# Plain float32 projections, eight weight tiles in the ring, and the later conditioning on TensorE

## Chip, cores and metric

The kernel runs on one core of a Trainium2 chip. The metric is the device time of one execution in microseconds, as the median of several runs.

## What is computed

One layer of an encoder for 256 tokens of width 1024, in float32, with a conditioning vector c:

```python
h = rmsnorm(x) * (1 + scale1(c)) + shift1(c)
proj = h @ w_in                      # 1024 x 6688
x = x + gate1(c) * (concat(gdn_heads(proj), ssd_heads(proj)) @ w_out)   # 2048 x 1024
h = rmsnorm(x) * (1 + scale2(c)) + shift2(c)
x = x + gate2(c) * moe(h)            # 32 experts, top 4 of them for each token
out = rmsnorm(x)
```

The six conditioning vectors are c times a 1024 x 6144 matrix. The eight GDN heads (gated delta rule) and sixteen SSD heads work on chunks of the sequence, after a causal convolution over four tokens and a SiLU. Every expert has 12 MiB of weights, and all 32 are read.

## The kernel before

The front computes everything up to the router and the experts follow. Weights come in tiles of 1 MiB (128 partitions x 2048 columns). The names in `SLOTS` are 20 such places in SBUF; in the front five of them (`w0` to `w4`, `RING`) are a ring for weights, and the others hold working data. In the expert stage all twenty become one ring in the order of `SLOTS`: `fetch` loads expert weights into a place as soon as its last user is done. Two ring places that the front no longer needs are filled early (`Early`), six more after the GDN pairs, four after SSD, and the last eight when the front is over.

The front's weight work is a list of units, loaded in that order through SP's queue (`issue` loads the next one whose place is free). A unit `Ada` is 256 columns of the conditioning matrix, `Win` 256 columns of `w_in` with two jobs of 128 columns, `Wout` a part of `w_out` with two jobs. The first eight `Ada` units give shift1 and scale1, and two `Win` units go beside them. The other 16 `Ada` units (`pieces`) stand one after each of the next `Win` units.

The projections are in fp32r, with each operand split into a part that fp32r holds and the remainder, and three products for one: `Job.split` copies the weights (ScalarE, L323) and subtracts (GpSimd, L327, two instructions a job); h is split as `hs` (L675, L676) and y as `ys` (L1007, L1008, L1172, L1173). The multiplications of `Win` are on L363, those of `Wout` on L449. `Ada.run` has two ways: on TensorE (L386, the first eight) or on VectorE (L390, L392, the 16 pieces), eight operations of 128 x 256 each; `fill` puts them between the jobs, two at a time (`between`). `ada_cols` (L408) and `ada_rows` (L416) bring a piece's sums to columns or spread them over all partitions.

GDN (`gdn_pair`, four pairs of heads, 27 steps each) and SSD (`ssd`) are generators that yield after each step, and `run` calls the `filler` in between, so that half jobs of the projections stand between the steps (in the trace parts of a half job stand there too: the order on an engine is set when the program is built):

```python
for pr in range(4):
    run(gdn_pair(pr), (20, 32, 44, 52)[pr], 27)
...
run(ssd(), 62, 26)
```

After a job `post` does the convolution (`conv`: ScalarE L538 and L542, VectorE L540 three times and L545) or a gate (`gate2`), from one of two PSUM banks (`pmm`). `rsqrt` (L265 to L270) is a chain of eleven small VectorE operations; each pair has two of them, each SSD group one. `issue_after` queues instructions behind a given one on its engine. Ten small loads of biases and gates (`chores`) are issued from GpSimd's queue between the jobs.

Of the kernel before, what the change touches and what calls it, by code (L numbers as in the profile page):

```python
# [41 lines left out]
RING = 5  # L42

SLOTS = ("w0", "w1", "g", "odd", "c", "hh", "hl", "s2", "s1", "even", "xd", "s3", "w2", "w3", "w4", "wh", "wl", "yh",
# [4 lines left out]
def trunk_kernel(ctx: ExitStack, tc: tile.TileContext, x, c, ada_w, ada_b, norm1_g, norm2_g, w_in,  # L49
# [102 lines left out]
    whs, wls = slot("wh", "whs", FR), slot("wl", "wls", FR)  # L152
# [154 lines left out]
    def run_all(gen):  # L307
        for _ in gen:
            pass

    units, issued, done, oacc, free = [], [0], [0], [], set()
    class Job:
# [5 lines left out]
        def split(self, dst=None):  # L318
            u, i = self.unit, self.i
            w = u.half(i)  # L320
            h = turn("wh") * 1024
            self.wh, self.wl = (v[:, h:h + 1024] for v in dst or (whs, wls))
            self.first = S.activation(u.shaped(self.wh), w, AF.Copy)  # L323
            wh, wl = u.shaped(self.wh), u.shaped(self.wl)
            q = w.shape[1] // 2
            for r in (slice(0, q), slice(q, 2 * q)):
                self.last = (V if dst else G).tensor_tensor(wl[:, r], w[:, r], wh[:, r], op=OP.subtract)  # L327
            if i:
                u.w = None
                issue(u.tag)  # L330

        def mm(self, part):
            self.unit.mm(self, part)

# [3 lines left out]
    class Win:  # L338
# [9 lines left out]
        def half(self, i):  # L348
            return self.w[:, :, ts(i)]

        def shaped(self, v):
            return v.rearrange("p (k m) -> p k m", k=KT)
# [15 lines left out]
    class Ada:  # L368
# [9 lines left out]
        def run(self, tensor=True):  # L378

            a = self.a = part("c", (0, 256, 1536, 1792)[turn("adas", 4)], [256])  # L380
            if tensor:
                p = pg()
                for i in range(2):
                    for j in range(4):
                        k = 2 * j + i
                        self.last = T.matmul(p[32 * j:32 * j + 32, :256], cact[:, k:k + 1].to_broadcast([128, 32]), self.w[:, k],  # L386
                                 start=(i == 0), stop=(i == 1))
                S.activation(a, p[:, :256], AF.Copy)
            else:
                V.tensor_scalar(a, self.w[:, 0], cact[:, 0:1], None, op0=OP.mult)  # L390
                for k in range(1, KT):
                    V.scalar_tensor_tensor(a, self.w[:, k], cact[:, k:k + 1], a, op0=OP.mult, op1=OP.add)  # L392
                    if k % 2 and k < KT - 1:
                        yield
# [5 lines left out]
            self.over = quarter if tensor else ones  # L400
            self.w = None
            issue(self.tag)

    def ada_cols(u, dst):

        p = pg()
        for i in range(2):
            last = T.matmul(p[:, i:i + 1], u.a[:, ts(i)], u.over[:, 0:1], start=True, stop=True)  # L408
# [11 lines left out]
    class Wout:  # L420
# [9 lines left out]
        def half(self, i):  # L430
            return self.w[:, 2 * i:2 * i + 2]

        def shaped(self, v):
            return v.rearrange("p (k m) -> p k m", k=2)

        def mm(self, job, t):
            wh, wl = self.shaped(job.wh), self.shaped(job.wl)
# [36 lines left out]
    def fill():  # L474

        todo, sums, late = None, [], []
# [5 lines left out]
        def between():  # L482
            if sums:
                try:
                    next(sums[0][0])
                except StopIteration:
                    late.append([1, sums.pop(0)[1]])

        for j in jobs:
            if isinstance(j, Ada):  # L490
                sums.append((j.run(False), j))
# [3 lines left out]
            between()  # L495
# [7 lines left out]
            if n < len(real):  # L503
                real[n].split()
# [1084 lines left out]
```

## Time and profile before

| | us |
|---|---|
| median of 3 runs | 1420.82 (1420.29 to 1422.03) |
| the profiled execution | 1424.03 |
| its span, first to last instruction | 1422.2 |
| TensorE busy | 1272.2 |
| VectorE busy | 627.0 |
| ScalarE busy | 246.4 |
| GpSimd busy | 210.3 |

The profile is of one execution. PE is TensorE's multiplications, PEld its loads of the stationary operand, DVE VectorE, ACT ScalarE, POOL GpSimd, SP the engine whose queue issues most loads (SPq: an issue). Times stand in us from the start of the span, or ns where a row says so. A line such as L363 is a line of the kernel.

### The profile page before, as it was taken

The numbers are of one execution on the slowest core, as the hardware profiler recorded it, in microseconds if no ns is written. First come the engines' busy times: TensorE is split into PE (matmuls) and PEld (weight loads), VectorE is DVE, ScalarE is ACT, GpSimd is POOL, SyncE is SP. The second block draws the span as 40 slices with busy tenths as digits, with TensorE's granted clock in tenths as the row PEclk, the third lists the DMA queues.
The fourth block names the chain that finished last, engine by engine and source line by source line (L and its number), as shares of the span: only waits on it lengthen the run. The fifth ranks groups of instructions, "written<-read, shape, count | busy, mean of one in ns | idle before, by whom it ended". The sixth has DMA issues, their size and how long they took to land. (4 is left out here: it accounts for less than half of the span.)

```text
span 1422.2 us, 20287 instructions
## 1 busy us (share of the span) xinstructions
PE 1272.2 (89%) x8024; PEld 662.7 (47%) x8025; DVE 627.0 (44%) x1586; ACT 246.4 (17%) x464; POOL 210.3 (15%) x185
## 2 busy tenths in 40 slices
PE   5889698889888899999999999899998799999996
PEld 3777687788666333333333323233333333333332
DVE  6889998954686322323322322223222133222322
ACT  3343333342243000001000000001000010100001
POOL 3345443444464000000000000000000000000000
PEclk8989898999999999999999999999999899999997
DMA  9754455332628699999999999999999999999990
GB/s 340 240 168 162 155 159 177 110 129 86 240 90 319 276 424 423 422 424 424 424 423 422 424 424 423 423 423 424 424 424 424 424 424 424 381 423 424 422 409 33
DMA packets 130472, 469.78 MB, mean 330 GB/s; under 512 B 7900, under 2 KB 59216, under 8 KB 97568
## 3 DMA queue, kind: packets, MB, share of 16 engines
q1 hardware_dynamic: 128592, 464.58, 81.3%
q8 instruction: 95, 1.56, 0.4%
q0 software_dynamic: 1040, 1.67, 0.4%
q10 hardware_dynamic: 704, 1.64, 0.4%
q14 instruction: 41, 0.34, 0.1%
HBM read 466.22 MB, written 1.05 MB: 329 GB/s over the span
## 5 line engine op out<-in xcount | busy, mean ns | idle before, releaser
L1398 PE MATMUL pG<-w,xe 128*64 128x512 f32 (+1 forms) x1152 | 283.5, 579 | 21.3 <-DMA w<-in_moe_w_gu_dram 21.1
L1398 PE MATMUL pU<-w,xe 128*64 128x512 f32 (+1 forms) x1152 | 280.6, 574 | 0.0
L1426 PE MATMUL pY<-w,hTe 128*64 128x512 f32 x1024 | 225.2, 592 | 0.9 <-ACT hTe L1415 0.7
L1402 DVE TENSOR_SCALAR ga<-pG 128x512 f32<-128x512 f32 (+1 forms) x34 | 23.0, 676 | 411.8 <-PE pG L1398 411.8
L327 POOL TENSOR_TENSOR wls<-w,whs 128x512 fp32r<-128x512 f32 x128 | 170.0, 1350 | 216.5 <-ACT whs L323 205.8
L363 PE MATMUL mm<-hs,whs 128*128 128x256 f32 x800 | 174.1, 310 | 30.7 <-DVE t_c L540 13.1
L1398 PEld LDWEIGHTS pG<-w,xe 128*64 128x64 f32 (+1 forms) x1152 | 83.9, 135 | 163.1 <-issue 103.9
L1398 PEld LDWEIGHTS pU<-w,xe 128*64 128x64 f32 (+1 forms) x1152 | 87.9, 135 | 142.4 <-issue 139.9
L363 PEld LDWEIGHTS mm<-hs,whs 128*128 128x128 f32 x800 | 136.5, 207 | 37.7 <-issue 24.4
L1426 PEld LDWEIGHTS pY<-w,hTe 128*64 128x64 f32 x1024 | 71.8, 137 | 133.0 <-issue 127.9
L363 PE MATMUL mm<-hs,wls 128*128 128x256 f32 x400 | 121.8, 304 | 0.0
L1404 ACT ACTIVATE th<-ga 128x512 f32<-128x512 f32 (+1 forms) x34 | 21.1, 620 | 470.4 <-DVE ga L1402 470.4
L1437 DVE SCALAR_TENSOR_TENSOR ye<-pY,gs,g2p 128x512 f32<-128x512 f32 (+1 forms) x33 | 24.2, 734 | 172.7 <-PEq L1491 163.8
L323 ACT ACTIVATE whs<-w 128x1024 fp32r<-128x1024 f32 x66 | 69.8, 1058 | 84.6 <-PE mm L363 41.7
L363 PEld LDWEIGHTS mm<-hs,wls 128*128 128x128 f32 x400 | 82.8, 207 | 1.6 <-issue 0.7
L392 DVE SCALAR_TENSOR_TENSOR t_c<-w,cact,t_c 128x256 f32<-128x256 f32 x112 | 77.0, 697 | 0.2
L1370 DVE TENSOR_SCALAR xe<-pw,A,sh 128x64 f32<-128x64 f32 (+1 forms) x272 | 70.9, 337 | 0.5 <-PE pw L1366 0.5
L1438 ACT ACTIVATE yh<-ye 128x512 fp32r<-128x512 f32 (+1 forms) x35 | 21.2, 607 | 281.3 <-DVE ye L1437 277.3
L1357 PE MATMUL pw<-xt,P 128*64 128x512 f32 (+1 forms) x288 | 66.0, 592 | 0.0
L1395 PE MATMUL pG<-bias,id 96*64 96x512 bf16 (+1 forms) x72 | 14.6, 394 | 27.7 <-PEq L1491 27.7
L1360 ACT ACTIVATE xg<-pw 128x512 f32<-128x512 f32 (+1 forms) x34 | 19.9, 585 | 110.3 <-PE pw L1357 110.3
L1377 DVE TENSOR_SCALAR QT<-pU 128x256 fp32r<-128x256 f32 x32 | 13.6, 425 | 53.5 <-PE pU L1373 53.4
(444 smaller groups left out, 1345.9 us busy)
## 6 DMA issues: line engine op xcount, KB each, us to landing
w<-in_moe_w_gu_dram SPq DMA_DIRECT2D x256, 1024.0 KB, 19.4
w<-in_moe_w_down_dram SPq DMA_DIRECT2D x127, 1024.0 KB, 19.6
w<-in_w_in_dram SPq DMA_DIRECT2D x26, 1024.0 KB, 5.4
w<-in_ada_w_dram SPq DMA_DIRECT2D x24, 1024.0 KB, 5.3
w<-in_w_out_dram SPq DMA_DIRECT2D x8, 1024.0 KB, 4.8
xt<-in_x_dram ACTq DMA_DIRECT2D x1, 1024.0 KB, 5.3
w<-in_moe_w_down_dram SPq DMA_DIRECT2D x2, 512.0 KB, 17.8
out_dram<-o SPq DMA_DIRECT2D x4, 256.0 KB, 2.0
```

The source lines that it names most:

```text
L323: self.first = S.activation(u.shaped(self.wh), w, AF.Copy)
L327: self.last = (V if dst else G).tensor_tensor(wl[:, r], w[:, r], wh[:, r], op=OP.subtract)
L363: T.matmul(job.p, a[:, k], hs[b][:, k], start=(k == 0 and j == 0), stop=(k == KT - 1 and j == 2))
L392: V.scalar_tensor_tensor(a, self.w[:, k], cact[:, k:k + 1], a, op0=OP.mult, op1=OP.add)
L1357: T.matmul(p[self.rows(h), :self.wid], self.P[:, t], xt[:, t, self.cols(h)], start=(t == 0), stop=(t == 1))
L1370: V.tensor_scalar(xe[:, k], p[:, c0:c0 + cap], A2[:, k:k + 1], sh2[:, k:k + 1], op0=OP.mult, op1=OP.add)
L1398: self.last = T.matmul(dst, self.xe[:, k], self.w(k)[:, o:o + wid], start=False, stop=(k == KT - 1))
L1402: V.tensor_scalar(ga, self.pG, 7.0, None, op0=OP.min)
L1404: S.activation(th, ga, AF.Tanh, scale=0.851)
L1426: T.matmul(pY[self.rows(n)], self.hT[:, k % self.nt, self.rows(k // self.nt)], self.w(8 + k // 2)[:, k % 2, self.cols(n)], start=False, st ...
L1437: V.scalar_tensor_tensor(ye[:, c], self.pY[:, c], self.gs, g2p[self.cap][:, c], op0=OP.mult, op1=OP.mult)
L1438: S.activation(self.yh[:, c], ye[:, c], AF.Copy)
```

## The change

Both projections and the small one of L731 multiply float32 operands as they are: one multiplication where there were three, and no splits of weights, h or y. The weight tile of a unit is released after the last multiplication of its second job. The four places of splits (`hh`, `hl`, `wh`, `wl`) go; three become ring tiles (`RING` 8) and one holds h (`hT`). All 24 `Ada` units run on TensorE. Five ring places are filled early with expert weights, five more after the pairs. The ten small loads go through SP's queue.

```diff
-RING = 5
-
-SLOTS = ("w0", "w1", "g", "odd", "c", "hh", "hl", "s2", "s1", "even", "xd", "s3", "w2", "w3", "w4", "wh", "wl", "yh",
+RING = 8
+
+SLOTS = ("w5", "w6", "w7", "w0", "w1", "g", "odd", "c", "hT", "s2", "s1", "even", "xd", "s3", "w2", "w3", "w4", "yh",
          "yl", "xT")
...
-    whs, wls = slot("wh", "whs", FR), slot("wl", "wls", FR)
...
-        def split(self, dst=None):
-            u, i = self.unit, self.i
-            w = u.half(i)
-            h = turn("wh") * 1024
-            self.wh, self.wl = (v[:, h:h + 1024] for v in dst or (whs, wls))
-            self.first = S.activation(u.shaped(self.wh), w, AF.Copy)
-            wh, wl = u.shaped(self.wh), u.shaped(self.wl)
-            q = w.shape[1] // 2
-            for r in (slice(0, q), slice(q, 2 * q)):
-                self.last = (V if dst else G).tensor_tensor(wl[:, r], w[:, r], wh[:, r], op=OP.subtract)
-            if i:
-                u.w = None
-                issue(u.tag)
...
         def mm(self, part):
             self.unit.mm(self, part)
+            if part and self.i:
+                self.unit.release()
...
+        def release(self):
+            self.w = None
+            issue(self.tag)
...
         def mm_k(self, job, ks):
-            wh, wl = self.shaped(job.wh), self.shaped(job.wl)
             for k in ks:
-                for j, (a, b) in enumerate(((wh, 0), (wh, 1), (wl, 0))):
-                    T.matmul(job.p, a[:, k], hs[b][:, k], start=(k == 0 and j == 0), stop=(k == KT - 1 and j == 2))
+                T.matmul(job.p, self.w[:, k, ts(job.i)], hT[:, k], start=(k == 0), stop=(k == KT - 1))
...
-        def run(self, tensor=True):
...
-            if tensor:
-                p = pg()
-                for i in range(2):
-                    for j in range(4):
...
-                S.activation(a, p[:, :256], AF.Copy)
-            else:
-                V.tensor_scalar(a, self.w[:, 0], cact[:, 0:1], None, op0=OP.mult)
-                for k in range(1, KT):
-                    V.scalar_tensor_tensor(a, self.w[:, k], cact[:, k:k + 1], a, op0=OP.mult, op1=OP.add)
-                    if k % 2 and k < KT - 1:
...
-                if self.rows:
-                    o = 1024 + turn("rows") * 512
-                    self.parts = wbx[:, o:o + 512].rearrange("p (i n) -> p i n", i=2)
-                    S.activation(self.parts[:, 0], a, AF.Copy)
-                    V.tensor_tensor(self.parts[:, 1], a, self.parts[:, 0], op=OP.subtract)
...
+            p = pg()
+            for i in range(2):
+                for j in range(4):
+                    k = 2 * j + i
+                    self.last = T.matmul(p[32 * j:32 * j + 32, :256], cact[:, k:k + 1].to_broadcast([128, 32]),
+                                         self.w[:, k], start=(i == 0), stop=(i == 1))
+            S.activation(a, p[:, :256], AF.Copy)
             self.w = None
             issue(self.tag)
...
         p = pg()
-        for i in range(2):
-            T.matmul(p[:, :256], ones_r, u.parts[:, i], start=(i == 0), stop=(i == 1))
+        T.matmul(p[:, :256], quarter, u.a, start=True, stop=True)
...
             for i in range(2):
                 k = k0 + i
-                y = ys[self.kp][:, :, k % 4]
-                for j, (a, b) in enumerate(((0, wh), (0, wl), (1, wh))):
-                    T.matmul(oacc[self.nn][t], y[:, a, ts(t)], b[:, i], start=(k == 0 and j == 0),
-                             stop=(k == 15 and j == 2))
+                T.matmul(oacc[self.nn][t], ys[self.kp][:, k % 4, ts(t)], self.w[:, 2 * job.i + i], start=(k == 0),
+                         stop=(k == 15))
...
-        real = [None] * 4 + [j for j in jobs if isinstance(j, Job)]
-        real[4].split()
         n = 4
...
         for j in jobs:
             if isinstance(j, Ada):
-                sums.append((j.run(False), j))
+                j.run()
+                late.append([2, j])
                 continue
             if todo:
                 todo()
-            between()
...
-            if n < len(real):
-                real[n].split()
             if n >= 6 and n % 2 == 0 and chores:
-                with tc.issue_after(real[n].last.ins):
+                with tc.issue_after(last_load[0].ins):
                     chores.pop(0)()
-            between()
...
-    for u, i in zip(units, (4, 2, 1, 3, 4, 2, 3, 4)):
+    for u, i in zip(units, (2, 3, 4, 5, 6, 7, 2, 3)):
...
-    hT = slot("yl", "hT").rearrange("p (k m) -> p k m", k=KT)
+    hT = slot("hT", "hT").rearrange("p (k m) -> p k m", k=KT)
...
-        for j in pre[2 * i:2 * i + 2]:
-            if j.k == 0:
-                j.split(wx if i else (whs, wls))
         for j in pre[2 * i:2 * i + 2]:
             j.unit.mm_k(j, range(j.k, k))
             j.k = k
+        if k == KT:
+            j.unit.release()
...
-            last = (S.activation(hs[0][:, k], hT[:, k], AF.Copy),
-                    V.tensor_tensor(hs[1][:, k], hT[:, k], hs[0][:, k], op=OP.subtract))
...
-        for j, (a, b) in enumerate(((0, 0), (0, 1), (1, 0))):
-            T.matmul(p[0:32, :SEQ], wbh[:, a, k], hs[b][:, k], start=(k == 0 and j == 0), stop=(k == KT - 1 and j == 2))
+        T.matmul(p[0:32, :SEQ], wbd[:, k], hT[:, k], start=(k == 0), stop=(k == KT - 1))
...
-        yf = y.rearrange("p c h l -> p (c h l)")
-        V.tensor_tensor(yf, yf, p, op=OP.mult)
-        for hp in range(2):
-            yhl = ys[pr // 2][:, :, pr % 2 * 2 + hp]
-            S.activation(c4(yhl[:, 0]), y[:, :, hp], AF.Copy)
-            V.tensor_tensor(c4(yhl[:, 1]), y[:, :, hp], c4(yhl[:, 0]), op=OP.subtract)
+        V.tensor_tensor(ys[pr // 2][:, pr % 2 * 2:pr % 2 * 2 + 2].rearrange("p h (c l) -> p c h l", c=4), y,
+                        p.rearrange("p (c h l) -> p c h l", c=4, h=2), op=OP.mult)
...
-        chores.append(lambda: nc.gpsimd.dma_start(dst, ada_b[:, c0:c0 + dst.shape[1]].to_broadcast(list(dst.shape))))
+        chores.append(lambda: nc.sync.dma_start(dst, ada_b[:, c0:c0 + dst.shape[1]].to_broadcast(list(dst.shape))))
...
-        chores.append(lambda: nc.gpsimd.dma_start(bf[32 * i:32 * i + 32], src))
+        chores.append(lambda: nc.sync.dma_start(bf[32 * i:32 * i + 32], src))
...
-                    V.scalar_tensor_tensor(xT[:, ct], xT[:, ct], sng[:, ct:ct + 1], p[:, 0:256],
+                    V.scalar_tensor_tensor(ys[2 + g][:, ct % 4], xT[:, ct], sng[:, ct:ct + 1], p[:, 0:256],
                                            op0=OP.mult, op1=OP.mult)
-                    yhl = ys[2 + g][:, :, ct % 4]
-                    S.activation(yhl[:, 0], xT[:, ct], AF.Copy)
-                    V.tensor_tensor(yhl[:, 1], xT[:, ct], yhl[:, 0], op=OP.subtract)
...
+    for tag in ("yh", "yl"):
+        v = slot(tag, "ys").rearrange("p (q k m) -> p q k m", q=2, k=4)
+        ys += [v[:, 0], v[:, 1]]
...
-    fetch(len(W) + 6)
+    fetch(len(W) + 5)
```

## Rows read from the trace of the kernel before

**Rows 1.** The page: bandwidth in 40 equal slices of the span.
```profile
GB/s 340 240 168 162 155 159 177 110 129 86 240 90 319 276 424 423 422 424 424 424 423 422 424 424 423 423 423 424 424 424 424 424 424 424 381 423 424 422 409 33
```

**Rows 2.** Windows by stage: busy us and instructions of each engine.
```profile
core 0: us, PE busy (x) PEld busy (x) DVE busy (x) ACT busy (x) POOL busy (x), PEclk, DMA share, GB/s
...
49.20:72.00 22.80, 15.96 (x116) 15.04 (x116) 21.15 (x67) 7.06 (x17) 9.77 (x9) 0.85 0.59 189
72.00:166.00 94.00, 77.45 (x770) 70.78 (x769) 84.65 (x181) 33.67 (x68) 47.72 (x40) 0.91 0.50 164
166.00:244.00 78.00, 65.25 (x664) 58.90 (x664) 72.69 (x161) 29.79 (x58) 36.67 (x30) 0.91 0.51 163
244.00:317.00 73.00, 62.93 (x667) 56.80 (x666) 56.83 (x130) 27.94 (x55) 31.94 (x25) 0.96 0.36 120
317.00:369.00 52.00, 47.66 (x529) 41.22 (x527) 24.13 (x64) 15.87 (x32) 25.32 (x20) 0.97 0.33 112
369.00:437.00 68.00, 56.64 (x311) 42.31 (x309) 54.39 (x93) 24.77 (x40) 38.05 (x30) 0.95 0.48 178
437.00:452.00 15.00, 13.76 (x72) 10.21 (x70) 8.25 (x17) 6.95 (x19) 8.03 (x6) 1.00 0.76 293
452.00:476.00 24.00, 17.02 (x68) 8.29 (x70) 12.15 (x61) 2.25 (x7) 0.00 (x0) 0.79 0.57 233
476.00:496.00 20.00, 19.72 (x96) 7.01 (x94) 5.75 (x15) 1.83 (x3) 0.00 (x0) 1.00 0.96 386
```

**Rows 3.** TensorE's waits, 49.2 to 452 us: total, times, longest.
```profile
PE mm L363 <- DVE t_c L540: 13.1, 7, 4.0
PE mm L363 <- DVE pl L768: 6.8, 1, 6.8
PE mm L363 <- DVE rot L268: 5.9, 2, 4.5
PE g L1141 <- DVE t_s L1124: 5.4, 4, 2.2
PE iv L921 <- DVE t_s L936: 4.7, 6, 1.5
PE g L1002 <- DVE roy L270: 4.7, 3, 1.7
PE mm L363 <- DVE rkt L268: 4.4, 1, 4.4
```

**Rows 4.** The page: groups by line; busy us, mean ns, idle before.
```profile
L327 POOL TENSOR_TENSOR wls<-w,whs 128x512 fp32r<-128x512 f32 x128 | 170.0, 1350 | 216.5 <-ACT whs L323 205.8
...
L392 DVE SCALAR_TENSOR_TENSOR t_c<-w,cact,t_c 128x256 f32<-128x256 f32 x112 | 77.0, 697 | 0.2
```

**Rows 5.** Window of dense fp32r projections of 256 columns, L363 alone.
```profile
55.13:59.92 4.79, 4.59 (x39) 4.38 (x37) 1.00 1.00 329
```

**Rows 6.** Window of dense fp32r projections of 512 columns, L449 alone.
```profile
435.52:439.50 3.98, 3.82 (x17) 2.81 (x15) 1.00 1.01 415
```

**Rows 7.** Lines one by one: duration ns min/median/max, first and last start.
```profile
L1096 PE MATMUL g<-xe,t_s x4: 590/592/592, 376.9 to 378.2; 128*128 128x512 f32 x4
...
L540 DVE SCALAR_TENSOR_TENSOR t_c<-mm,cwg,t_c x72: 465/470/484, 61.3 to 282.6; 128x255 f32<-128x255 f32 x24, 128x254 f32<-128x254 f32 x24, 128x253 f32<-128x253 f32 x24
...
L270 DVE SCALAR_TENSOR_TENSOR roy<-rot,roy x12: 147/160/1214, 155.1 to 366.7; 128x4 f32<-128x4 f32 x12
```

**Rows 8.** Timeline of SP's queue around the start of the experts.
```profile
439.69 15.96 SPq L87 DMA_DIRECT2D w<-in_moe_w_gu_dram  x8
475.97 0.39 SPq L87 DMA_DIRECT2D w<-in_moe_w_down_dram  x1
```

**Rows 9.** Timeline: a conditioning piece on TensorE, and a pair's end.
```profile
36.95 1.07 PE L386 MATMUL g<-w,cact 128*32 128x256 f32 x16
...
306.36 1.29 POOL L327 TENSOR_TENSOR wls<-w,whs 128x512 fp32r<-128x512 f32 x1 [3.00 <-ACT whs L323]
...
306.51 1.17 DVE L265 TENSOR_SCALAR roy<-vv 128x4 int32<-128x4 int32 x1
```

More of the change, by code (lines that the diff above doesn't have):

```diff
@@ L304, in trunk_kernel @@
     sh2 = const.tile([128, KT], FT)
-    def run_all(gen):
-        for _ in gen:
-            pass
     units, issued, done, oacc, free = [], [0], [0], [], set()
@@ L346, in load @@
             self.w = load(win_src[:, :, self.c0:self.c0 + 256], [KT, 256], self.tag, self in loads[:10])
[L348 to L352, printed above, removed]
+        def release(self):
+            self.w = None
+            issue(self.tag)
         def mm(self, job, part):
@@ L376, in load, with run @@
             self.w = load(ada_src[:, :, self.c0:self.c0 + 256], [KT, 256], self.tag, self in loads[:10])
-        def run(self, tensor=True):
+        def run(self):
             a = self.a = part("c", (0, 256, 1536, 1792)[turn("adas", 4)], [256])
-            if tensor:
-                p = pg()
-                for i in range(2):
-                    for j in range(4):
-                        k = 2 * j + i
-                        self.last = T.matmul(p[32 * j:32 * j + 32, :256], cact[:, k:k + 1].to_broadcast([128, 32]), self.w[:, k],
-                                 start=(i == 0), stop=(i == 1))
-                S.activation(a, p[:, :256], AF.Copy)
-            else:
-                V.tensor_scalar(a, self.w[:, 0], cact[:, 0:1], None, op0=OP.mult)
-                for k in range(1, KT):
-                    V.scalar_tensor_tensor(a, self.w[:, k], cact[:, k:k + 1], a, op0=OP.mult, op1=OP.add)
-                    if k % 2 and k < KT - 1:
-                        yield
-                if self.rows:
-                    o = 1024 + turn("rows") * 512
-                    self.parts = wbx[:, o:o + 512].rearrange("p (i n) -> p i n", i=2)
-                    S.activation(self.parts[:, 0], a, AF.Copy)
-                    V.tensor_tensor(self.parts[:, 1], a, self.parts[:, 0], op=OP.subtract)
-            self.over = quarter if tensor else ones
+            p = pg()
[5 more added lines that the diff above has]
+            S.activation(a, p[:, :256], AF.Copy)
             self.w = None
@@ L407, in ada_cols @@
         for i in range(2):
-            last = T.matmul(p[:, i:i + 1], u.a[:, ts(i)], u.over[:, 0:1], start=True, stop=True)
+            last = T.matmul(p[:, i:i + 1], u.a[:, ts(i)], quarter[:, 0:1], start=True, stop=True)
         V.tensor_tensor(dst, p[:, 0:2], col("ab", 48)[:, u.c0 // 128:u.c0 // 128 + 2], op=OP.add)
@@ L428, in load, with release @@
             self.w = load(wout_src[:, 4 * self.kp:4 * self.kp + 4, self.nn * 512:self.nn * 512 + 512], [4, 512], self.tag, True)
[L430 to L434, printed above, removed]
+        def release(self):
+            self.w = None
+            issue(self.tag)
         def mm(self, job, t):
-            wh, wl = self.shaped(job.wh), self.shaped(job.wl)
             k0 = 4 * self.kp + 2 * job.i
@@ L474, in fill @@
     def fill():
-        todo, sums, late = None, [], []
+        todo, late = None, []
         jobs = [j for u in units[KT + 2:] if not isinstance(u, Early) for j in (u.jobs or [u])]
-        real = [None] * 4 + [j for j in jobs if isinstance(j, Job)]
-        real[4].split()
         n = 4
[L482 to L487, printed above, removed]
         for j in jobs:
             if isinstance(j, Ada):
-                sums.append((j.run(False), j))
+                j.run()
+                late.append([2, j])
                 continue
@@ L516, in finish_ada @@
         u = Ada(c0, None)
-        u.rows = kind is ada_rows
         u.finish = lambda: kind(u, dst)
@@ L631, in trunk_kernel @@
         issue(f"w{i}")
-    hs = [slot(tag, "hs", FR).rearrange("p (k m) -> p k m", k=KT) for tag in ("hh", "hl")]
     pre = [j for u in units[KT:KT + 2] for j in u.jobs]
@@ L639, in trunk_kernel @@
         j.p, j.k = p[:, :SEQ], 0
-    wx = [slot(tag, "wx", FR) for tag in ("s2", "g")]
     def pre_run(i, k):
-        for j in pre[2 * i:2 * i + 2]:
-            if j.k == 0:
-                j.split(wx if i else (whs, wls))
         for j in pre[2 * i:2 * i + 2]:
@@ L654, in trunk_kernel @@
         for i, u in enumerate(ua):
-            run_all(u.run())
+            u.run()
             if 2 * k2 + i == 6:
@@ L722, in trunk_kernel @@
     wbx = slot("xd", "wbh", FR)
-    wbh = wbx[:, 0:512].rearrange("p (a k m) -> p a k m", a=2, k=KT)
-    with tc.issue_after(last[0].ins):
-        S.activation(wbh[:, 0], wbd, AF.Copy)
-    with tc.issue_after(last[1].ins):
-        V.tensor_tensor(wbh[:, 1], wbd, wbh[:, 0], op=OP.subtract)
     p = pg()
     for k in range(KT):
-        for j, (a, b) in enumerate(((0, 0), (0, 1), (1, 0))):
-            T.matmul(p[0:32, :SEQ], wbh[:, a, k], hs[b][:, k], start=(k == 0 and j == 0), stop=(k == KT - 1 and j == 2))
+        T.matmul(p[0:32, :SEQ], wbd[:, k], hT[:, k], start=(k == 0), stop=(k == KT - 1))
     bd = fr.tile([32, 4, 2, 64], FT, name="bd", tag="rot", bufs=3)
@@ L819, in gdn_pair @@
         kT, qT, vT = (pair_tile(pr, n) for n in ("kT", "qT", "vT"))
-        rg = wbx[:, 512:1024].rearrange("p (i n) -> p i n", i=2)
+        rg = wbx[:, 0:512].rearrange("p (i n) -> p i n", i=2)
         for i, E in enumerate((V, G)):
```

5 lines of the change are left out of this document (removed).

## The prediction

> **What bounds the kernel now.** I read the bandwidth line of the page first: from about 480 us on the transfers run at 422 to 424 GB/s to the end [rows 1]. The expert stage is a stream of weights and the edit doesn't touch it, so it can only start earlier or later. The load queue shows which: its eight first-round loads of expert weights are issued by 455.65 us, and the next is issued at 475.97 us, when expert 0 has used up its first tile [rows 8]; the DMA share in between is 0.57 and then 0.96 [rows 2]. All 20 tiles are full before the experts start. So the end moves one for one with the end of the front, and loading 14 tiles early in place of 12 buys nothing.
>
> Next the windows of the front, 49.2 to 452 us (402.8 us) [rows 2]. TensorE is busy 339.7 us of it and idle 63.1. In the three stages from 72 to 317 VectorE is busy 214 of 245 us; from 317 to 369, where no conditioning piece is left, 24 of 52, and TensorE's idle share falls from 16% to 8%. The waits say who holds it: the seven shown, 45.0 us, all end with VectorE, most of them in front of a projection whose PSUM bank waits for a convolution or for the small operations queued ahead of it [rows 3]. The front is therefore a TensorE program held up by a full VectorE queue, in which GpSimd also has 170 us of weight splits [rows 4].
>
> **TensorE's added work.** The price of the two forms comes from dense stretches at the full clock. 39 fp32r multiplications of 256 columns start in 4.79 us, 0.12 us each [rows 5]; 17 of 512 columns in 3.98 us, 0.234 each [rows 6]. A float32 multiplication stands as two instructions: the four of L1096 (two multiplications, 512 columns) start from 376.9 to 378.2 us, three steps of 0.43 us [rows 7]. No row shows 256 columns on a full stationary tile. In proportion it is 0.214 us an instruction; an upper bound is 0.24, twice the fp32r step. I take 0.214, since the 512-column row leaves nearly nothing fixed per instruction.
>
> - Input projections: 52 jobs of eight k steps. 24 x 0.12 = 2.88 us becomes 16 x 0.214 = 3.42: +0.54, in all +28.
> - Output projection: 16 jobs. 12 x 0.234 = 2.81 becomes 8 x 0.428 = 3.42: +0.61, in all +10.
> - The 32-column projection of L731: 24 x 0.12 to 16 x 0.214, +0.5.
> - Sixteen pieces of conditioning on TensorE: 16 instructions took 1.07 us in the first eight pieces at full clock [rows 9], so 16 x 1.0 = +16. Four 32-column strips run side by side there, hence so little.
> - The eight row pieces spread with float32 in place of two fp32r: +0.2 each, +1.5.
>
> Sum: +56 us of TensorE time. Nothing of TensorE's own work goes away.
>
> **What is taken from the others.** VectorE loses the 112 multiply-adds of L392, 77 us [rows 4], the sixteen L390 that open the pieces, and the remainder subtractions of h, y and the row pieces: at least 77 of the 322 us that it is busy from 49.2 to 452 [rows 2]. GpSimd loses the whole of L327, 170 us. ScalarE loses the 66 copies of L323 and gains 16 short ones; it is never busy for half of a stage [rows 2], so neither counts.
>
> The splits cost more than their own time. VectorE's 4-element L270 takes 0.16 us at the median and 1.21 at worst, but L540, which reads PSUM, only 0.465 to 0.484 [rows 7]; at 306.4 us an L265 that works on 4 elements took 1.17 us just as L327 was running on GpSimd [rows 9]. Eleven such operations in a row stand at each end of a pair, and TensorE waits 4.7 us in front of L1002 and 5.9 and 4.4 in front of projections behind them [rows 3], 15 us in all. With no L327 they should be near their medians; what GpSimd keeps (its shares of rg, eg and ra) is a few microseconds a pair.
>
> The Trainium skill (SBUF — State Buffer, the part on the two sides and the shared port pair) says that VectorE and GpSimd have one port pair in common, that whoever starts first holds it for a whole instruction, and that the other is blocked fully; the rows on L270 and L540 agree. By that rule the 15 us of waits at the pair ends go; were the stretch something else, they would stay, and the sum would be +7 and not -8.
>
> **What TensorE can get back.** First the idle 63 us. Then the clock: its mean in the six stages before 437 us is 0.85, 0.91, 0.91, 0.96, 0.97 and 0.95 [rows 2], which makes 54 us at 1.2 GHz. Much of that is the idle time itself; taking half of it as work, which then took twice as long as it would, 13 us are lost. Together 76 us.
>
> How much returns decides the sign. With VectorE at 24 of 52 us but GpSimd still splitting, the stage from 317 to 369 us kept 8% idle [rows 2]. That is the bound from above: 33 us of idle in some 400, and 5 of clock. The bound from below is nothing left. After the edit the convolutions are still there, some 55% of VectorE in the pairs, but the pair ends lose their stretched operations and each half job in between covers 1.7 us in place of 1.4. I take 10 us of idle and 2 of clock left: 64 come back. 56 - 64 = -8.
>
> **What costs nothing, and under what cover.** Eight ring tiles: in the first slice the loads already run at 340 GB/s [rows 1] and their order stays, and after 49.2 us no wait for a load is among the seven [rows 3]. Were a load late, TensorE would stand for its 5 us. A tile is now released by its last multiplication, not by its split, so it is held about a job (3.4 us) longer; three more tiles cover that. The ten small loads move from GpSimd's queue to SP's. There each stands behind loads that wait for a tile; who needs them (bias parts, row pieces) comes jobs later. If one were late, it would hold a VectorE addition, and all convolutions behind it. The wait of a piece for two jobs, not one, before its columns are used delays nothing that is read before the front's end. Dropping the split of h takes a ScalarE and a VectorE step out of the first stage, but the four early jobs are longer by 0.54 each, which the +28 holds.
>
> **Sum.** The profiled execution took 1424.0 us (span 1422.2), 3.2 over the median 1420.8. 1424 - 8 = 1416, so 1413 as a median. A change within 0.2% (2.8 us) can't be told from none.
>
> **Rivals.**
>
> 1. TensorE becomes the bound and its idle time stays (slower). If pairs keep the 8% of the stage from 317 to 369, 38 of 76 us come back: 56 - 38 = +18, 1439. It decides from 56 us on, that is when more than 20 of the 76 are left. For it: that stage had little VectorE work and was still not full. Against: it had GpSimd's splits. Chance 0.25 for anything that ends slower this way, most of it near +8 to +12.
> 2. Everything comes back, and gaps too short to show as idle (a projection starts some 0.1 us late after a small multiplication) are hidden under the longer instructions: -20 to -25, 1396 to 1401. Chance 0.13.
> 3. The gain is eaten: no change, 1418 to 1424. The pair ends keep half of their 15 us (4.7, 5.9 and 4.4 [rows 3]), because L270 and its like stay stretched beside GpSimd's other work or queue behind convolutions: -8 + 7.5. Chance 0.12.
> 4. The price of 256 columns is the upper bound: 0.026 x 16 x 52 = +21 on the forecast, 1434. The rows for 512 columns speak against it. Chance 0.08. The Trainium skill (FP8 and Floating Point Precision, on true FP32) counts four passes through the array; by four fp32r steps of 0.12 that is 0.48 us for 256 columns, this rival's price, while L1096's 0.856 us for 512 is less than four times 0.234.
>
> **How the numbers follow.** The forecast holds 0.42, with a range of its own from 1405 to 1419 (0.40 of it faster, 0.02 same). Rival 1 is 0.22 slower and 0.03 same, rival 3 is 0.09 same, 0.02 faster and 0.01 slower, rival 2 all faster, rival 4 all slower. Faster 0.40 + 0.13 + 0.02 = 0.55, same 0.14, slower 0.31. The range of eight in ten reaches from the second rival to the middle of the first: 1397 to 1432.
>
> **What would show it.** Right: projections at 0.21 us an instruction with 832 of them in the input projections; no L327; L270 near 0.16 us at its mean; TensorE idle 10 to 20 us between 50 and 450, clock 0.97 or more; SP's first load of the second round near 468 us in place of 475.97. Wrong: instructions of 0.24 us, or idle over 20 us behind convolutions; then that load comes after 476. If the experts start earlier and the total doesn't follow, the step from the front to the end was wrong.

## The result and the profile after

The changed kernel takes 1396.06 us at the median of four runs (1392.94 to 1398.35), the kernel before 1420.74 (1420.29 to 1422.03): a ratio of 0.9817, with a 95% interval of 0.98 to 0.9834. The forecast was 1413, its own range 1405 to 1419. By its number what came is the second rival, "everything comes back", at 1396 to 1401, and it lies 1 us under the low end of the whole range. The profiled execution took 1398.35 us, its span 1396.5.

First the bandwidth line of the changed kernel's page, in slices of 34.9 us (35.6 before). It answers to [rows 1]:

```profile
GB/s 340 277 237 139 180 190 182 122 91 116 216 211 197 422 425 424 424 423 422 424 424 424 424 424 423 425 424 424 422 424 424 417 423 424 372 423 423 422 394 31
```

The full stream of about 424 GB/s starts one slice earlier and is as fast as before. So the gain lies ahead of it. The windows of the changed kernel by stage, with the columns of [rows 2]:

```profile
core 0: us, PE busy (x) PEld busy (x) DVE busy (x) ACT busy (x) POOL busy (x), PEclk, DMA share, GB/s
...
49.20:72.00 22.80, 22.80 (x121) 17.11 (x120) 12.55 (x58) 6.45 (x20) 0.62 (x1) 1.00 0.95 331
72.00:166.00 94.00, 93.79 (x864) 72.27 (x864) 56.02 (x160) 25.76 (x65) 4.50 (x3) 1.00 0.58 193
166.00:244.00 78.00, 77.96 (x719) 59.67 (x717) 40.94 (x112) 18.32 (x45) 3.58 (x3) 1.00 0.53 173
244.00:317.00 73.00, 72.93 (x676) 58.39 (x675) 36.70 (x102) 16.35 (x41) 5.66 (x5) 1.00 0.30 102
317.00:345.00 28.00, 27.84 (x214) 20.81 (x213) 10.29 (x33) 3.78 (x10) 0.00 (x0) 1.00 0.25 83
```

The second number of a row is its length, the next TensorE's busy time: 0.5 us of 295.8 are left idle, at the full clock (2.4 GHz) throughout. Before, TensorE had 0.85 to 0.97 of the clock here and idle time in every stage [rows 2]. GpSimd, busy for 126 us of the four stages from 49.2 to 317 us before, is busy for 14. What is left of TensorE's waits, from 49.2 to 425 us:

```profile
PE g L1167 <- ACT x1T L1165: 0.7, 1, 0.7
PE g L937 <- DVE roy L269: 0.4, 2, 0.2
PE g L1072 <- DVE t_s L1055: 0.3, 1, 0.3
```

Of the seven waits of [rows 3], 45.0 us, one is left, at a tenth: L937 is the old L1002, which waited 4.7 us and now waits 0.4. From 49.2 to 345 us TensorE's own work sets the front's length.

To compare kernels whose stages have moved, one window is taken in all that follows: from 49.2 us to the first instruction of the routing tables (the first L1349 of the kernel before, 462.36 us; in each other kernel up to 0.4 us before the same instruction). The row of the kernel before, then of the changed kernel:

```profile
49.20:462.36 413.16, 348.87 (x3149) 300.31 (x3148) 328.48 (x748) 147.70 (x290) 197.49 (x158) 0.93 0.48 164
```

```profile
49.20:434.62 385.42, 383.06 (x2966) 275.81 (x2964) 206.78 (x600) 86.95 (x221) 22.85 (x20) 1.00 0.52 181
```

The front is 27.7 us shorter with 34.2 us more of busy TensorE in it. The load queue's first load of the second round is at 448.35 us in place of 475.97 [rows 8]:

```profile
448.35 0.39 SPq L87 DMA_DIRECT2D w<-in_moe_w_down_dram  x1
```

### The profile page after: what moved, and what is told of

Its sections match the earlier page's. It is cut to its first block, busy times and chain, and to the rows that moved or that the text cites. A ratio compares the mean times of both kernels' runs of the same rounds, so it can differ in the third digit from the quotient of the medians.

```text
span 1396.5 us, 19286 instructions
## 1 busy us (share of the span) xinstructions
PE 1306.4 (94%) x7792; PEld 634.9 (45%) x7793; DVE 494.2 (35%) x1417; ACT 176.4 (13%) x379; POOL 34.7 (2%) x47
## 5 line engine op out<-in xcount | busy, mean ns | idle before, releaser
L342 PE MATMUL mm<-hT,w 128*128 128x256 f32 x800 | 202.6, 394 | 0.0
L1323 PEld LDWEIGHTS pG<-w,xe 128*64 128x64 f32 (+1 forms) x1152 | 83.3, 135 | 164.4 <-issue 101.0
L342 PEld LDWEIGHTS mm<-hT,w 128*128 128x128 f32 x800 | 145.6, 193 | 27.3 <-issue 7.2
L487 DVE SCALAR_TENSOR_TENSOR t_c<-mm,cwg,t_c 128x255 f32<-128x255 f32 (+2 forms) x72 | 34.5, 479 | 21.6 <-ACT t_c L485 20.6
L364 PE MATMUL g<-w,cact 128*32 128x256 f32 x384 | 33.5, 443 | 7.2 <-DMA w<-in_ada_w_dram 4.9
L1375 PE MATMUL acc<-yh,QT 64*128 64x512 f32 (+1 forms) x148 | 33.5, 430 | 3.2 <-ACT yh L1363 3.2
L1285 ACT ACTIVATE xg<-pw 128x512 f32<-128x512 f32 (+1 forms) x34 | 19.9, 585 | 109.6 <-PE pw L1282 109.6
L1320 PEld LDWEIGHTS <-id 96*64 96x64 bf16 (+1 forms) x144 | 5.9, 106 | 56.5 <-PEq L1416 52.5
L1282 PEld LDWEIGHTS pw<-xt,P 128*64 128x64 f32 (+1 forms) x288 | 17.1, 135 | 30.8 <-issue 30.1
```

The costliest lines, as they stand in the source:

```text
L342: T.matmul(job.p, self.w[:, k, ts(job.i)], hT[:, k], start=(k == 0), stop=(k == KT - 1))
L487: V.scalar_tensor_tensor(acc[:, s:], p[:, :SEQ - s], wc(3 - s), acc[:, s:], op0=OP.mult, op1=OP.add)
L1282: T.matmul(p[self.rows(h), :self.wid], self.P[:, t], xt[:, t, self.cols(h)], start=(t == 0), stop=(t == 1))
L1323: self.last = T.matmul(dst, self.xe[:, k], self.w(k)[:, o:o + wid], start=False, stop=(k == KT - 1))
L1375: T.matmul(dst, self.QT[n % 2][half_, t], part[half_, i * w:(i + 1) * w], start=False, stop=part is self.yl, skip_group_check=True)
```

## The experiments

Three theories of why so much came back. (A) VectorE lost the multiply-adds of the conditioning pieces. (B) GpSimd lost the subtractions of the split, which had stretched VectorE's work. (C) The longer float32 projections cover the gaps. Times are medians; ratios are to the kernel before, measured side by side (its medians there: 1420.3 to 1421.4).

**The pieces alone.** The kernel before, its 16 later pieces on TensorE, splits kept:

```
...
             if isinstance(j, Ada):
-                sums.append((j.run(False), j))
+                run_all(j.run())
+                late.append([2, j])
                 continue
```

> The kernel before with one part of the change alone: the 16 later pieces of the conditioning on TensorE; splits and the ring of five stay. Three theories of why 83 us of TensorE's time came back. (A) VectorE: with the multiply-adds of the pieces gone, its queue no longer holds TensorE. Then idle time of 49 to 450 us falls from 63 to under 20 us, TensorE has 16 us more to do, and the time falls by 25 to 35 us, to 1386 to 1396. (B) GpSimd: the subtractions of the split stretch VectorE's operations through a shared resource. They are still there, so over 40 us of idle time stay and the time is 1415 to 1435. (C) Cover: the longer float32 projections hide the gaps. They are not there either: 1420 to 1437.

Measured: 1413.96 us, 0.9942 (0.9924 to 0.9961). The front's row:

```profile
49.20:457.04 407.84, 364.09 (x3391) 302.43 (x3388) 261.73 (x609) 148.71 (x296) 190.01 (x156) 0.94 0.48 167
```

VectorE is 67 us less busy, and TensorE still has 44 us of idle time, where (A) wanted under 20 and (B) over 40. The time is 1 us under (B)'s range. A queue that is a fifth emptier does not end the waits.

**The pieces back.** The changed kernel with the pieces on VectorE in their old places (the old branch of `run`, its steps put between the half jobs):

```
             if isinstance(j, Ada):
-                j.run()
-                late.append([2, j])
+                if True:
+                    sums.append((j.run_v(), j))
...
                 continue
```

> The changed kernel with the 16 later pieces back on VectorE, in the places they had before; projections in plain float32, eight ring tiles. TensorE has 16 us less to do than in the changed kernel, VectorE about 90 us more (some 290 of 376). (A) VectorE's load made the idle time: 35 us or more of it return, 1412 to 1430. (B) and (C): with no subtraction on GpSimd, or with the longer projections as cover, idle time stays under 8 us and the time falls by 10 to 16 us, to 1380 to 1388.

Measured: 1376.26 us, 0.9677 (0.964 to 0.9714), 20 us faster than the changed kernel (4 us more than (B) and (C) allowed), and the fastest version here that leaves nothing of the computation out. Its front, and the multiply-adds in its lines of VectorE from 49 to 470 us (busy us, mean ns, idle before):

```profile
49.20:413.97 364.77, 360.42 (x2706) 266.65 (x2704) 248.81 (x725) 80.47 (x205) 21.92 (x20) 1.00 0.55 189
```

```profile
L362 DVE SCALAR_TENSOR_TENSOR t_c<-w,cact,t_c 128x256 f32<-128x256 f32 x111 | 53.1, 479 | 1.1
```

(A) falls: with the pieces on VectorE TensorE is idle for 4.3 us only. The same instruction took 697 ns on average before [rows 4]; here it takes 479. The pieces were never a load of 77 us; 24 of that was waiting inside the instruction.

**No subtractions.** The kernel before, all multiplications kept, the remainders of the later weights zero:

```
...
-            for r in (slice(0, q), slice(q, 2 * q)):
-                self.last = (V if dst else G).tensor_tensor(wl[:, r], w[:, r], wh[:, r], op=OP.subtract)
+            if dst:
+                for r in (slice(0, q), slice(q, 2 * q)):
+                    self.last = V.tensor_tensor(wl[:, r], w[:, r], wh[:, r], op=OP.subtract)
+            else:
+                self.last = self.first
```

> The kernel before without the subtractions that form the remainders of the later weights (the remainders are set to zero once, so that part of the product is left out); all multiplications, ScalarE's copies and the pieces on VectorE stay. (A) VectorE still has its multiply-adds: 0 to -10 us, 1410 to 1421. (B) GpSimd's 170 us were what stretched VectorE: idle falls by 30 us or more, 1380 to 1393, and the four-element operations fall to their median of 0.16 us. (C) 0 to -5 us.

Measured: 1350.28 us, 0.9505 (0.9462 to 0.9547), 30 us below the range of (B), which was right in kind and far too small.

```profile
49.20:387.72 338.52, 327.50 (x3175) 284.01 (x3174) 252.94 (x749) 148.56 (x293) 22.88 (x20) 0.99 0.58 200
```

This is theory (B) alone: the short projections are still there, the pieces are still on VectorE, and the front falls by 74.6 us (the times by 70.7, at the medians; the profiled execution of the kernel before was 3 us over its median). VectorE has as many instructions as before (749 and 748 recorded) and is busy 75.5 us less. Instruction by instruction, with the medians of this run as the measure: 447 of VectorE's in the kernel before meet none of GpSimd's and take 0.4 us less in all, while the 299 that meet one take 87 us more. The stretch is therefore time beside GpSimd, and the rows of the kernel before showed it as busy. TensorE's busy time falls as well, by 21.4 us, with the same multiplications and the granted clock at 0.99 in place of 0.93. Busy time times clock is 324 us in both, so by this estimate all of it is what the low clock had cost.

**Half the subtractions.** The kernel before, with the first of the two subtractions of a job kept:

```
-            for r in (slice(0, q), slice(q, 2 * q)):
+            for r in (slice(0, q), slice(q, 2 * q)) if dst else (slice(0, q),):
```

> The kernel before with one of GpSimd's two subtractions per job left out (half of each remainder stays zero). If the loss goes by GpSimd's busy time, about half of the 70 us comes back: 1380 to 1392. If the queue has a threshold (TensorE covers the first half): 1350 to 1365. If only the last subtraction of a job counts, because TensorE waits for it: 1400 to 1421.

Measured: 1382.5 us, 0.9736 (0.9698 to 0.9775).

```profile
49.20:421.50 372.30, 338.36 (x3149) 292.80 (x3148) 287.80 (x746) 146.76 (x290) 111.22 (x94) 0.95 0.53 183
```

GpSimd's busy time is 22.9, 111.2 and 197.5 us in the three kernels, the front 338.5, 372.3 and 413.2: 33.8 us for the first half, 40.9 for the second. So the loss goes on average by GpSimd's busy time, some 0.43 us of the front for each of its microseconds, and TensorE covers no first part of it.

**Subtractions that nobody reads.** TensorE might simply have waited for the remainder. So all are made, and the third product reads the high part again (on L449 likewise):

```
-                for j, (a, b) in enumerate(((wh, 0), (wh, 1), (wl, 0))):
+                for j, (a, b) in enumerate(((wh, 0), (wh, 1), (wh, 1))):
```

> The kernel before with all of GpSimd's subtractions, but TensorE's third product reads the other operands' high part again, so that nothing reads the remainders of the weights (the product with the remainder is left out and the one with the low part of h, or the high part of the weights with the low part of y, is taken twice). If GpSimd's work itself is the loss, through VectorE: 1410 to 1425, as before. If TensorE's wait for the remainder is the loss: 1350 to 1370, as without subtractions.

Measured: 1417.63 us, 0.9972 (0.995 to 0.9994): 4 us of the 71, at the medians. The wait for the data is next to nothing; GpSimd's work itself is the loss. (The two profiled fronts, 400.0 and 413.2 us, lie further apart, since these executions took 1413.23 and 1424.03 us.)

```profile
49.20:449.16 399.96, 341.18 (x3152) 294.31 (x3151) 327.29 (x748) 147.53 (x290) 198.93 (x158) 0.95 0.49 171
```

**Subtractions put into the changed kernel.** Four tries, each with two subtractions of 128x512 per job that no computation uses. The first:

```
+            if done[0] < 51:
+                for r in (slice(1024, 1536), slice(1536, 2048)):
+                    G.tensor_tensor(wbx[:, r], xt[:, 0, 0:512], xt[:, 1, 0:512], op=OP.subtract)
             j.mm(1)
```

> The changed kernel with GpSimd made to do 94 subtractions of 128x512 that nobody reads, two per projection job as in the split. (A) VectorE has room: 0 to +5 us over the changed kernel, 1396 to 1401. (B) VectorE's operations are stretched again: +20 us or more, 1416 or more, with idle time at the pair ends. (C) the longer projections hide it: 0 to +8 us.

Measured: 1488.86 us (1477.84 to 1500.09), 1.0496 (1.042 to 1.0571), over 80 us more than the changed kernel, but not as (B) meant it. The timeline of GpSimd from 14 us, then of VectorE from 38 to 135 (start, us, instruction, idle before), and L616 as a whole (minimum, median, maximum in ns, first and last start in us):

```profile
15.18 115.75 POOL L459 TENSOR_TENSOR wbh<-xt 128x512 fp32r<-128x512 f32 x94
```

```profile
42.69 0.16 DVE L375 TENSOR_TENSOR sh<-g,cols 128x2 f32<-128x2 f32 x1 [8.37 <-PE g L374]
43.14 0.16 DVE L375 TENSOR_TENSOR A<-g,cols 128x2 f32<-128x2 f32 x1 [0.29 <-PE g L374]
43.33 87.62 DVE L616 SCALAR_TENSOR_TENSOR A<-A,cols 128x2 f32<-128x2 f32 x1
```

```profile
L616 DVE SCALAR_TENSOR_TENSOR A<-A,cols x4: 481/662/87625, 18.0 to 43.3; 128x2 f32<-128x2 f32 x4
```

Nothing held the subtractions to the jobs, so all 94 ran in one row. L375 reads PSUM for one operand and took its 0.16 us in the middle of them. L616 is two elements wide with both operands in SBUF. It ran four times beside the row. Three times it took 0.48 to 0.78 us and ended some 0.02 us after the subtraction that it had met. The fourth time it took 87.62 us: it ended when the row did. TensorE waited 83.2 us for what came behind it.

The second try names the job's first half as what each pair is issued behind. That did not hold them either, for `issue_after` queues behind an instruction of the same engine, and the one named is TensorE's:

```
                 for r in (slice(1024, 1536), slice(1536, 2048)):
+                    with tc.issue_after(j.unit.last.ins):
```

> The changed kernel with the same 94 subtractions of 128x512 on GpSimd, but each pair let go only after the first half of its job's multiplications, so that they lie two per job as the splits did. If GpSimd's instruction blocks VectorE's for as long as it runs, whatever covers it, idle time of TensorE returns: +10 to +40 us, 1406 to 1436, and VectorE's 4-element operations are stretched to about 1.2 us. If only subtractions without a gap between them block it (as in the run with all of them in one row), or if the longer projections are cover enough: 0 to +4 us.

Measured: 1493.31 us, 1.0518 (1.0469 to 1.0568): again all 94 in a row, 115.70 us, and the same two-element operation beside them, here L617. It repeats the run above and tells nothing of the question it was made for.

```profile
L617 DVE SCALAR_TENSOR_TENSOR A<-A,cols x4: 163/426/98447, 18.4 to 138.6; 128x2 f32<-128x2 f32 x4
```

In the third, ScalarE reads two columns of the last pair before the next pair may overwrite them:

```
+                S.activation(seen, wbx[:, 1024:2048].rearrange("p (a b) -> p a b", a=2)[:, :, 0], AF.Copy)
```

> The changed kernel with 94 subtractions of 128x512 on GpSimd that no computation uses, and this time really held to two per projection job: a short ScalarE instruction reads the last pair's result in each job before the next pair may overwrite it. If a GpSimd instruction blocks VectorE for as long as it runs, and VectorE's queue then holds TensorE: +10 to +45 us over the changed kernel, 1406 to 1441. If the longer projections cover it: 1396 to 1400.

Measured: 1467.0 us, 1.0326 (1.0284 to 1.0367), and inconclusive: the reads ran ahead of the jobs as well, two subtractions every 2.8 us, and TensorE waited for ScalarE's queue in which they stood:

```profile
PE g L374 <- ACT t_c L366: 26.5, 4, 11.6
PE g L680 <- ACT bd L677: 7.4, 1, 7.4
```

In the fourth TensorE reads each pair's result at the end of its job:

```
             j.mm(1)
+            if isinstance(j.unit, Win) and n in made:
+                T.matmul(j.full[:, 256:264], made[n][:, 0:128].bitcast(FT), hT[:, 0, 0:8], start=True, stop=True)
```

> The changed kernel with two subtractions of 128x512 on GpSimd per projection job, held to the jobs by data this time: TensorE reads eight columns' worth of the pair's result at the end of its job, into a part of the job's PSUM bank that nothing uses, and two buffers take turns, as the remainders did. If GpSimd's blocking of VectorE costs TensorE as much per GpSimd microsecond as in the kernel before (70 us for 170), some 118 us of it cost 40 to 50 us: 1436 to 1446. If VectorE's free time (200 of 375 us busy) and the longer projections take half of it: 1410 to 1425. If they take all: 1396 to 1402.

Measured: 1428.22 us, 1.0057 (1.004 to 1.0075), 32.2 over the changed kernel. GpSimd's timeline shows that they now come with the jobs, and its lines of 49 to 464 us what they took:

```profile
72.79 2.62 POOL L441 TENSOR_TENSOR wbh<-xt 128x512 fp32r<-128x512 f32 x2 [3.73 <-PE mm L470]
76.47 2.62 POOL L441 TENSOR_TENSOR wbh<-xt 128x512 fp32r<-128x512 f32 x2 [1.06 <-PE mm L470]
```

```profile
L441 POOL TENSOR_TENSOR wbh<-xt 128x512 fp32r<-128x512 f32 x88 | 112.9, 1284 | 198.2 <-PE mm L470 194.8
```

```profile
49.20:464.37 415.17, 397.41 (x3055) 293.37 (x3054) 226.64 (x600) 87.15 (x221) 136.01 (x108) 0.98 0.48 167
```

TensorE's 92 small added instructions take 9.3 us from start to start; 23 us remain for 112.9 of GpSimd, 0.20 us for each, where it was 0.43. None of TensorE's waits in the front ends with GpSimd, so this is no wait for the pair that it reads. Without the 9.3 us the time is 1419, the middle case: an emptier VectorE queue and longer projections take about half of the blow. Which of the two takes how much was not separated, but VectorE's busy time is up by only 19.9 us (226.64 against 206.78), about what the front lost. That speaks for the emptier queue: fewer of its instructions met one of GpSimd's.

**The subtractions on VectorE.** The kernel before with `V` in place of `G`:

```
+        def rest(self):
...
-                self.last = (V if dst else G).tensor_tensor(wl[:, r], w[:, r], wh[:, r], op=OP.subtract)
+                self.last = V.tensor_tensor(wl[:, r], w[:, r], wh[:, r], op=OP.subtract)
```

> The kernel before with the remainders of the later weights formed on VectorE in place of GpSimd; pieces of the conditioning stay on VectorE. Theory that GpSimd's place cost the 70 us, not the work: VectorE gets 128 subtractions of about 0.68 us, 87 us more on the 246 us of the run without subtractions, 333 us in a front that then took 328: VectorE becomes the bound, but the time still falls, to 1370 to 1400. Rival, that VectorE's load is what counts: slower than before, over 1425.

Measured: 1411.29 us, 0.9938 (0.9916 to 0.9959). Not slower, as the rival had it, but 11 us over the theory's range: by the times neither was right. Lines of VectorE from 49 to 450 us, and the front:

```profile
L333 DVE TENSOR_TENSOR wls<-w,whs 128x512 fp32r<-128x512 f32 x128 | 85.9, 685 | 10.5 <-ACT whs L323 10.3
L398 DVE SCALAR_TENSOR_TENSOR t_c<-w,cact,t_c 128x256 f32<-128x256 f32 x112 | 56.7, 506 | 0.1
```

```profile
49.20:449.50 400.30, 356.38 (x3187) 303.83 (x3185) 330.32 (x881) 150.07 (x293) 23.91 (x20) 0.94 0.49 170
```

VectorE's 330 us were forecast to 3 us; that TensorE would keep up beside a queue 82% full was the error: 44 us of idle time. How much of it is the queue's load, and how much that each job now waits for a subtraction in it, is open.

**And the pieces on TensorE.** This change and that of the first experiment in one kernel:

```
+                self.last = V.tensor_tensor(wl[:, r], w[:, r], wh[:, r], op=OP.subtract)
...
+                run_all(j.run())
```

> The same, and the 16 later pieces on TensorE: TensorE 318 + 16 = 334 us, VectorE about 280. If both are right and VectorE is no bound: 1358 to 1372, under the 1376 of plain float32 with the pieces on VectorE, since TensorE then has 19 us less to do. If the order of VectorE's queue holds the projections (each now waits for a remainder): 1376 to 1400.

Measured: 1389.17 us, 0.9784 (0.9744 to 0.9825), the second case: TensorE has less to do than in plain float32 and 23 us of idle time.

```profile
49.20:426.00 376.80, 353.91 (x3431) 295.80 (x3429) 281.93 (x744) 151.41 (x301) 23.59 (x20) 0.98 0.51 179
```

So a full VectorE queue does cost TensorE time, and here (A) has its truth: 22 us between these two runs. It is only not what the change gained most by.

**Ring of five.** The changed kernel with five tiles, and so two expert tiles loaded early into the ring:

```
-RING = 8
...
+RING = 5
...
```

> The changed kernel with five ring tiles in place of eight, and two expert tiles loaded into them early in place of five. Theory: the ring and the early loads buy nothing, since the load queue waits for expert 0 in either case: 1393 to 1400. Rival: with a tile held a job longer, loads come late in front of the projections, or the stream of the experts starts with fewer tiles: 1401 to 1415.

Measured: 1395.7 us, 0.9825 (0.9785 to 0.9865): no difference from eight.

## Why the forecast was 17 us off

**The end follows the front: right.** The front is 27.7 us shorter, the span 25.7. What lies behind this window takes 959.8 us before and 961.9 after; over the twelve experiments it lies between 958 and 963, so the 2 us are scatter. The load near 468 us came at 448.35, because the front was shorter than forecast, not by another mechanism. Loading 14 tiles early bought nothing, as said (ring of five).

**TensorE's added work: right to a few microseconds.** The kernel without subtractions has the instructions of before and hardly a low clock: 327.50 us. The changed kernel has 383.06: +55.6, where the sum was +56. That it fits so well is partly luck: at a clock of 0.99 some 3 us of the 327.50 are still the clock's, and single terms are off both ways. The sixteen pieces take 18.7 us in the changed kernel, from start to start (eleven 1.00 each, five with other work between their instructions 1.54), where 16 were taken; the spreading of the row pieces takes 3.9 us against 4.3, where +1.5 was taken. The largest term holds. Projections of 256 columns, L342 alone in a dense stretch of the changed kernel:

```profile
59.20:65.80 6.60, 6.31 (x30) 5.51 (x30) 1.00 0.80 285
```

Thirty in 6.60 us is 0.22 at the most (the median step from start to start is 0.216); the proportional value of 0.214 was the right end of the two, and the rival of 0.24 is gone. The Trainium skill (FP8 and Floating Point Precision, on true FP32) counts four passes through the array. That count is not refuted: what failed is to price a pass at the fp32r step of 0.12 us [rows 5], which made 0.48 us for 256 columns. Measured are two instructions of 0.216, 0.43 us, a quarter of which is 0.108.

**What TensorE gets back: the step that failed.** "Together 76 us ... 64 come back." By the run without subtractions it was 413.2 - 327.5 = 85.7 us, and 2.4 are left in the changed kernel (385.42 - 383.06): 83.3 came back. The forecast missed 19.3 us here, in two places. The clock: 13 us were taken for it, 21.4 were busy time that went with the subtractions. That half of the 54 us at 1.2 GHz was work was a choice without a row behind it. Work takes twice as long there, so the 21.4 lost stand for some 43 us (an estimate). And the rest that stays: 12 us were taken, 2.4 stayed. 56 - 83.3 is the 27 us of the front.

**Behind the second lies a misreading.** The port between VectorE and GpSimd was named and given the 15 us of the waits at the pair ends. GpSimd's subtractions in fact cost some 70 us (74.6 of the profiled front, 70.7 at the medians, 4 of it TensorE's wait for the data), all over the front. The rows to see it were there: L392 had a mean of 697 ns [rows 4] and an idle time before it of 0.2 us, while L540, which reads PSUM, stayed between 465 and 484 [rows 7]. The trace of the kernel before also has the minimum, median and maximum of L392 in ns:

```profile
L392 DVE SCALAR_TENSOR_TENSOR t_c<-w,cact,t_c x112: 387/479/1999, 45.0 to 278.8; 128x256 f32<-128x256 f32 x112
```

The median of 479 beside the mean of 697 tells that some took far longer than their work. The forecast did not use it, and L392 was counted as 77 us of work that the change removes from VectorE. Its work was 54 us (112 of 479 ns); the other 24 were standing beside GpSimd. The bound of 33 us of idle time came from the stage of 317 to 369, with the remark that GpSimd was still splitting there; it was busy for 25 of the 52 us [rows 2]. What those 25 us did to the 8% was not asked, and 10 us of idle time were taken between the bounds. In the changed kernel the stage of 317 to 345 has 0.16 us idle.

**The pieces.** The forecast credited VectorE's relief, most of it the pieces, with what came back. On their own they bring 7 us; with the subtractions gone, moving them to TensorE costs 20 us, for then TensorE is the bound and they are 18.7 us of its work. The change's gain of 25 us is a gain of 45 by all the rest, in which the ring has no part (1421.0 to 1376.26), and a loss of 20 by the pieces.

**Rivals.** Rival 1 (idle time stays) fell, by the argument that stood against it: its stage had GpSimd's splits. Rival 2 came by its number, but not by its reason. The short fp32r projections already give back all but 11 us of idle time once the subtractions are gone, so the longer ones can have covered no more than that; and beside GpSimd's work they take at most half of the loss (fourth try). Gaps too short to show as idle were looked for in no run. Rival 3, stretched operations at the pair ends beside GpSimd's other work, is not seen: the last operation of each step in `rsqrt`, 4 elements wide, on L269 of the changed kernel, minimum, median and maximum in ns:

```profile
L269 DVE SCALAR_TENSOR_TENSOR rky<-rkt,rky x12: 161/164/165, 88.7 to 302.2; 128x4 f32<-128x4 f32 x12
L269 DVE SCALAR_TENSOR_TENSOR roy<-rot,roy x12: 152/161/164, 151.0 to 344.6; 128x4 f32<-128x4 f32 x12
```

What costs nothing (the ring, the small loads, the wait of two jobs) cost nothing: no wait for a DMA is among TensorE's waits of the changed kernel from 49.2 to 425 us.

## What to carry to other kernels

Before VectorE's busy time is taken as work, compare the mean of its instructions with their median, and with those beside an idle GpSimd: here 75 of 328 us were waiting inside the instruction, and the front lost about as much. In this kernel a microsecond moved to GpSimd cost 0.2 to 0.4 us of a front that TensorE should have bound, and by these runs it is free only where no VectorE instruction that works on SBUF alone falls beside it. And take a change apart: of two parts that looked as if they served the same end, one gained 45 us and the other lost 20.

## What was not expected of the hardware

A waiting VectorE instruction can be passed over. Mostly it is let in as soon as the GpSimd instruction that it met has ended, also where the next one follows without a gap. Two timelines of the kernel before show either case, first GpSimd's two subtractions, then VectorE's instruction beside them:

```profile
87.78 2.55 POOL L327 TENSOR_TENSOR wls<-w,whs 128x512 fp32r<-128x512 f32 x2 [4.51 <-ACT whs L323]
87.82 1.28 DVE L268 TENSOR_TENSOR rkt<-rky 128x4 f32<-128x4 f32 x1
```

```profile
62.88 2.49 POOL L327 TENSOR_TENSOR wls<-w,whs 128x512 fp32r<-128x512 f32 x2
62.77 2.66 DVE L766 TENSOR_SCALAR pl<-s 128x48 f32<-128x48 f32 x1
```

L268 was done when the first subtraction was, in 1.28 us. L766 stood through both, 2.66 us. In the front of the kernel before, 68 of VectorE's instructions were stretched by over 0.2 us and met a seam of this kind (one GpSimd instruction ends, the next starts within 0.1 us); 62 were let in there. L616 was let in three times beside the row of 94 and then stood for 87.62 us, through 72 of them; L617 of the second try stood for 98.45. What decides it, no run here shows.

The Trainium skill (SBUF — State Buffer, the part on the two sides and the shared port pair) says that the holder keeps the pair for a whole instruction and that the loser is blocked fully. The runs agree, and go further, for the block can last over many instructions. That part of the Trainium skill names as VectorE's operations that contend those in a two-port mode, and those with two inputs in SBUF beside a GpSimd operation that reads it. The runs agree in that operations with an operand from PSUM are spared: L375 took 0.16 us within the row, and the convolutions' multiply-adds kept 465 to 484 ns beside the splits [rows 7].
